# Pair 3 instead of pair 2 by the seven-product scheme, the second norm's last two sums on VectorE, and its root ahead of a conversion

## The chip, the cores and the metric

The kernel runs on one core of a Trainium2 chip. The metric is the device time of one execution in microseconds (us). TensorE multiplies, VectorE, ScalarE and GpSimd do elementwise work (the profile calls the four PE, DVE, ACT and POOL), and SyncE (SP) issues most DMAs.

## The reference

One layer on a sequence of 512 positions with 1024 features: a norm, one wide projection, a short gated convolution beside causal attention, a gated merge added to x, then a second norm and a channel mixer, and a last norm. The change lies where the merge ends and the mixer begins:

```python
x = x + (g_conv * y_conv + g_attn * y_attn) @ w_o[l]
h = rms_norm(x, norm_ffn_g[l])                 # the second norm
up = causal_dwconv(h @ w_up[l], conv_ffn_w[l]) # 1024 -> 2 * 2816, three taps per feature
a, b = jnp.split(up, 2, axis=-1)
x = x + (jax.nn.silu(a) * b) @ w_down[l]
```

## The kernel before, in words

Features lie on the 128 partitions, positions along the free axis, so x is eight blocks of 128 x 512. To hold float32 accuracy every operand is split into a high and a low part (names ending in h and l), and a product takes three matmuls: high by high, low by high, high by low. Matmuls are 128 x 128 by 128 x 256.

**Weights.** All weights come through one list of chunks, `stream`, in the order of their use. SyncE loads a chunk into one of five `raw` buffers. `split` makes the two parts: ScalarE copies it to `wh_...` (line 267), and VectorE subtracts to get `wl_...` (line 271). There are two buffers for each part, so a chunk is split while the chunk before it is multiplied. Behind each split `run_later` hands out work that waits in the list `later`.

**The up projection.** `w_up` gives 44 blocks of 128 features. Blocks `up(2j)` and `up(2j+1)` make pair j: the a half and the b half of 128 hidden features. A plain pair takes two chunks of 1024 columns and 48 matmuls for each. The pairs in `UPS`, 2 and 7, go another way: `up_pair` multiplies two by two blocks by a scheme with seven products instead of eight (table `PROD`), from four chunks P, F, P, F whose sums were formed ahead in DRAM by accumulating DMAs (names `sum`). That is 84 matmuls for the pair instead of 96, but VectorE has to combine four results (lines 1068 to 1073). It also needs sums of x's blocks ("forms"): `x1_sums` makes them from the tiles `xs2`, in the steps `t13` (lines 977, 978), `t24` (981, 982) and `hl` (985 on ScalarE, 986 on VectorE), which leave the forms' two parts in `xf`. The other line numbers of a pair: the norm's factor at 1091, three taps at 603 (ScalarE), 604 and 607 (VectorE) into `fu`, silu at 1101, the product of the halves on GpSimd at 1104 (even pairs, `ge`) or 1111 (odd, `go`). Behind an odd pair the forms for the down projection are made from `ge` and `go` (lines 1121 to 1131).

**The second norm.** As each block j of `x1` comes out of the product with `w_o` (`xr`, line 1001), it is split to `x1h` and `x1l` (1002, 1003), squared on ScalarE (`sq2`, 933) and added to `ssq2` by GpSimd (934). At the end `ssq2` is split in two, `s20` (1019) and `s21` (1020). Two pairs of matmuls by a block of ones, `pc_n2` (1253), sum over the features. They stand in the midst of the first two up blocks: in `lead`, block up0 runs up to its seventh of eight, up1 up to its second, then `mid` is called with those sums, then the rest. Then come the root (1257, ScalarE) and the reciprocal (1258, VectorE) that give `rb_n2`, by which every up block is multiplied.

**What sets the order.** A scheduler orders each engine's instructions, within the order written for TensorE, SyncE and for what `keep` marks. `after_split` holds instructions behind the last split. The order below is the one that came out.

Of the kernel before, what the change touches and what calls it, by code (L numbers as in the profile page):

```python
# [8 lines left out]
F32 = mybir.dt.float32  # L9
F32R = mybir.dt.float32r  # L10
AF = mybir.ActivationFunctionType
ALU = mybir.AluOpType

P = 128
D = 1024
S = 512
KB = D // P
NT = S // P
# [35 lines left out]
HELD = 2  # L54
GS = 2
NFF = len(STEPS[0]) + len(STEPS[1])
UPS = (2, 7)
NUP = NFF + 2 * (8 - GS)

PLAIN = [(m, k) for m in (6, 7) for k in range(*PHASES[1])]  # L60
# [4 lines left out]
def block_kernel(ctx, tc, xT, vecs, wv, win, wmix, wo, wup, wst, wdp, outT):  # L65
# [3 lines left out]
    nc = tc.nc  # L69
    PSUM = bass.MemoryType.PSUM  # L70

    cp = ctx.enter_context(tc.tile_pool(name="cp", bufs=1))
# [3 lines left out]
    def keep(ins):  # L76
        return tc.keep_in_program_order(ins)

    def bank(i, name):
        return ps.tile([P, S], F32, tag=f"b{i}", name=name)  # L80

    def ring(*ids):
        st = [0]

        def f(name):
            st[0] += 1
            return bank(ids[(st[0] - 1) % len(ids)], name)

        return f
# [107 lines left out]
    later = []  # L197
    held = [0]

    def after_split():  # L200

        st = ExitStack()
        for ins in order.values():
            st.enter_context(tc.issue_after(ins))
        return st
# [29 lines left out]
    def flush(banks=None):  # L235

        while any(banks is None or set(w[2]) & set(banks) for w in later):
            with after_split():
                later.pop(0)[3]()
# [50 lines left out]
    halves = [slice(0, S // 2), slice(S // 2, S)]  # L290
# [33 lines left out]
    ex = cp.tile([P, NT + 2], F32, tag="ex", name="ex")  # L324
    nc.gpsimd.memset(ex[:, :NT], -0.5)
    eps = ex[:, NT : NT + 1]
# [118 lines left out]
    ssq = ct("ssq1")  # L445
# [338 lines left out]
    acc, bank_s, bank_t = ring(2, 0, 1), ring(3, 4), ring(5, 6)  # L784
# [3 lines left out]
    for idx in late:  # L788
        kind, i = divmod(idx, 4)
# [29 lines left out]
    acc = ring(3, 4, 5, 6, 0, 1, 2, 7)  # L819
# [6 lines left out]
    mp = mg.enter_context(tc.tile_pool(name="mp", bufs=1))  # L826
# [56 lines left out]
    for j in range(KB):  # L883
# [28 lines left out]
        a, b = gs  # L912
# [9 lines left out]
    x1h = xp.tile([P, KB, S], F32R, tag="x1h", name="x1h")  # L922
    x1l = xp.tile([P, KB * S + PADR], F32R, tag="x1l", name="x1l")[:, : KB * S]
# [1 line left out]

    ssq2 = xp.tile([P, S], F32, tag="ssq", name="ssq2")

    def square_into(ssq, x, first, pool, name):
        if first:
            nc.scalar.activation(ssq, x, AF.Square)  # L930
        else:
            sq = pool.tile([P, S], F32, tag="sq", name=name)
            nc.scalar.activation(sq, x, AF.Square)
            nc.gpsimd.tensor_add(ssq, ssq, sq)

    def lead(names, xh, xl, mid=None, late=None):

        w = [chunk(n) for n in names]
        p = [acc(f"p_{n}") for n in names]

        def part(i, kbs):
            for kb in kbs:
                ks = slice(kb * P, (kb + 1) * P)
                mm3(p[i], w[i][0][:, ks], w[i][1][:, ks], xh[:, kb, :], xl[:, kb, :], kb == 0, kb == KB - 1)

        part(0, range(KB - 1))
        part(1, range(2))
        if mid is not None:
            mid()
        part(1, range(2, 4))  # L950
        part(0, (KB - 1,))
        part(1, range(4, KB))
        if late is not None:
            late()
        return p
# [37 lines left out]
    for j in range(KB):  # L993
        if j == 0:
            po = lead(["wo0", "wo1"], mh, ml)
        p = po[j] if j < 2 else block(f"wo{j}", mh, ml)
        for i in range(len(xr), min(j + 3, KB)):
            xr.append(mt(f"xr{i}"))
            nc.gpsimd.dma_start(xr[i], xT[:, i, :])
        y = xr[j]  # L1000
        nc.vector.tensor_add(y, p, y)
        nc.scalar.activation(x1h[:, j, :], y, AF.Copy, scale=col(G2 + j))
        nc.vector.scalar_tensor_tensor(
            x1l[:, j, :], y, col(G2 + j), x1h.bitcast(F32)[:, j, :], op0=ALU.mult, op1=ALU.subtract,
        )
        square_into(ssq2, y, j == 0, mp, f"sq2_{j}")
        nc.gpsimd.dma_start(x1d[:, j, :], y)
        q, i = divmod(j, 2)
        if i == 0:
            xs2 = mp.tile([P, 4, 2 * P], F32, tag="xs2", name=f"xs2{q}", bufs=2)  # L1010
        nc.scalar.activation(xs2[:, 2 * i : 2 * i + 2].rearrange("p h c -> p (h c)"), y, AF.Copy, scale=col(G2 + j))
        if i:
            x1_sums(q, xs2)
    n2 = [mp.tile([P, S], F32R, tag="s2", name=f"s2{i}", bufs=2) for i in range(2)]
    n2.append(mp.tile([P, P], F32R, tag="one", name="one"))
    hl = later.pop()
    flush()
    nc.scalar.activation(n2[2], ones, AF.Copy)
    nc.scalar.activation(n2[0], ssq2, AF.Copy)
    nc.vector.tensor_sub(n2[1], ssq2, n2[0].bitcast(F32))  # L1020
    later.append(hl)
    flush()
    mg.close()
    ab.close()

# [7 lines left out]
    gl = fp.tile([P, NG, 2 * P], F32R, tag="gl", name="gl")  # L1033
    halves_of = "p (h c) -> p h c"

    acc = ring(0, 1, 4, 5, 6, 7, 2, 3)
    ssq3 = xp.tile([P, S], F32, tag="ssq", name="ssq3")

    def place(ph, q):
# [41 lines left out]
    def up(j, rb2, pu=None):  # L1081
        uu = []
        if j in UPS:
            pu = up_pair(j)
        for s_ in range(2):
            p = pu[s_] if pu else block(f"up{2 * j + s_}", x1h, x1l, True)
            z = p if j <= UPS[-1] else fz(f"fz{j}{s_}")
            if s_ and j in UPS:
                nc.vector.scalar_tensor_tensor(z, p, -1.0, rb2, op0=ALU.mult, op1=ALU.mult)
            else:  # L1090
                nc.vector.tensor_mul(z, p, rb2)
            u = fp.tile([P, S], F32, tag="fu", name=f"fu{j}{s_}", bufs=3)
            taps(u, z, CF + 3 * (2 * j + s_))
            uu.append(u)
        return uu

    def glu(ph, j, uu):
        a, b = uu
        q, k = j // 2, len(parts) - 1
        g0 = place(ph, q)  # L1100
        nc.scalar.activation(a, a, AF.Silu)
        if j % 2 == 0:
            ge = glu.even = fp.tile([P, 2, 2 * P], F32, tag="ge", name=f"ge{q}", bufs=2)
            keep(nc.gpsimd.tensor_mul(ge, a.rearrange(halves_of, h=2), b.rearrange(halves_of, h=2)))  # L1104
            return
        flush()
        ge = glu.even
        go = fp.tile([P, 6, 2 * P], F32, tag="gr", name=f"go{q}")

        def mul(eng):  # L1110
            return eng.tensor_mul(go[:, 0:2, :], a.rearrange(halves_of, h=2), b.rearrange(halves_of, h=2))

        if j + 1 < PHASES[ph][1]:
            keep(mul(nc.gpsimd))
        else:
            later.append((k + 3, 0.7, (("q", q),), lambda: mul(nc.vector)))
        b11, b12 = ge[:, 0, :], ge[:, 1, :]
        b21, b22, t1, t2, t3, t4 = (go[:, i, :] for i in range(6))

        def t13():  # L1120
            nc.vector.tensor_sub(t1, b11, b12)
            nc.vector.tensor_sub(t3, b22, b12)

        def t24():
            nc.vector.scalar_tensor_tensor(t2, t1, -1.0, b22, op0=ALU.mult, op1=ALU.subtract)
            nc.vector.scalar_tensor_tensor(t4, t2, -1.0, b21, op0=ALU.mult, op1=ALU.subtract)

        def hl(src, gs):
            def f():
                nc.scalar.activation(gh[:, gs, :], src, AF.Copy)  # L1130
                nc.vector.tensor_sub(gl[:, gs, :], src, gh.bitcast(F32)[:, gs, :])

            return f


        d = (2, 3, 4) if j + 1 < PHASES[ph][1] else (4, 5, 6)
        w = [(d[0], 0.85, t13), (d[0], 0.85, t24), (d[1], 0.7, hl(ge[:, : 1 + ph, :], slice(g0, g0 + 1 + NF * ph, NF)))]
        w += [(d[x > 0 and 2 or 1], 0.7, hl(go[:, x : x + 2, :], slice(g0 + 1 + x, g0 + 3 + x))) for x in (0, 4, 2)]
        for n, us, f in w:
            later.append((k + n, us, (("q", q),), f))  # L1140
# [99 lines left out]
    for ph, (j0, j1) in enumerate(PHASES):  # L1240
        if ph:
            flush()
            acc = ring(*X)
        for j in range(j0, j1):
            pu = None
            if j == 0:
                nrm = {}

                def mid():
                    pc = bank(6, "pc_n2")  # L1250
                    for i, x in enumerate(n2[:2]):
                        for c, cs in enumerate(halves):
                            keep(nc.tensor.matmul(
                                pc[:, cs], n2[2], x[:, cs], start=i + c == 0, stop=i + c == 2
                            ))
                    rb2 = cp.tile([P, S], F32, tag="rb", name="rb_n2")
                    nc.scalar.activation(rb2, pc, AF.Sqrt, bias=eps, scale=1.0 / D)
                    nc.vector.reciprocal(rb2, rb2)
                    nrm["b"] = rb2

                pu = lead(["up0", "up1"], x1h, x1l, mid)
            glu(ph, j, up(j, nrm["b"], pu))
        down(ph, ph * len(STEPS[0]))


# [210 lines left out]
```

## Time and profile before

| | us |
|---|---|
| median of 3 runs | 697.64 (697.44 to 698.34) |
| profiled execution | 697.58 |
| its span, first to last instruction | 695.5 |
| TensorE busy | 685.4 |
| VectorE busy | 536.3 |
| ScalarE busy | 359.3 |
| GpSimd busy | 167.1 |
| TensorE's granted clock, of full speed | 0.997 |

The profile is of one execution. A row of the order of time gives the start from the span's beginning, the duration, the engine, the line, the operation, the tiles without their numbers, the shapes, the count, and in brackets the idle time ahead of it on its engine and what ended it. TensorE's matmuls overlap, so their starts say more than their durations.

### The profile page before, as it was taken

What the parts mean: (1) busy time and instruction counts of PE and PEld (TensorE: products, weight loads), DVE (VectorE), ACT (ScalarE), POOL (GpSimd) and SP (SyncE); (2) the same over time, 40 slices, a digit from 0 to 9 for tenths busy, and PEclk for the clock granted to TensorE, in tenths of its full rate; (3) what the DMA queues carried; (4) which work ended last, traced back from release to release, by engine and by line L of the source; (5) the groups of instructions that cost most, each with busy time, mean ns of one, the idle gap of its engine ahead of it and who ended that gap; (6) DMA issues with size and microseconds to landing.
All of it is one profiled execution on the core that took longest, in us unless ns stands there. A gap on an engine that the chain in (4) does not pass through costs nothing.

```text
span 695.5 us, 14650 instructions
## 1 busy us (share of the span) xinstructions
PE 685.4 (99%) x5952; PEld 682.6 (98%) x5952; DVE 536.3 (77%) x842; ACT 359.3 (52%) x570; POOL 167.1 (24%) x194
## 2 busy tenths in 40 slices
PE   9999999999999999999999999999999999999996
PEld 9999999999999999999999999999999999999996
DVE  6678777786687778769889869987684678777786
ACT  6664656554654444456654535545433354445663
POOL 5124745444021020224410231340000221131000
PEclk9999999999999999999999999999999999999998
DMA  8526957478489697878658467579967273544723
GB/s 309 194 82 225 208 140 182 98 181 180 125 213 289 215 259 206 242 249 258 176 116 281 104 147 263 172 190 263 261 200 228 92 175 117 134 105 129 197 84 121
DMA packets 59202, 128.87 MB, mean 185 GB/s; under 512 B 5344, under 2 KB 26848, under 8 KB 58880
## 3 DMA queue, kind: packets, MB, share of 16 engines
q1 hardware_dynamic: 41280, 100.22, 44.0%
q0 software_dynamic: 17136, 27.04, 21.9%
q8 instruction: 46, 0.75, 0.4%
q10 hardware_dynamic: 720, 0.69, 0.3%
q14 instruction: 20, 0.16, 0.1%
HBM read 123.67 MB, written 41.42 MB: 237 GB/s over the span
## 4 chain that ended last, share of the span: by engine, by line
PE 85%; DVE 7%; ACT 4%; issue 3%; DMA 1%; ACTq 0%; SPq 0%; DVEq 0%
PE p_up L300 21%; PE p_in L300 14%; PE dn L318 13%; PE gs L318 8%; PE p_up L318 7%; PE yc L318 3%; PE ya L300 3%; PE us L318 2%; PE p_g L300 2%; PE o L693 2%; PE pa L512 1%; PE pb L514 1%; PE tp L678 1%; PE p_wo L300 1%; PE pdB L300 1%
## 5 line engine op out<-in xcount | busy, mean ns | idle before, releaser
L300 PE MATMUL p_in<-xf,wh_in 128*128 128x256 f32 x576 | 95.7, 278 | 0.0
L300 PE MATMUL p_up<-x1l,wh_up 128*128 128x256 f32 x488 | 95.2, 276 | 0.0
L300 PE MATMUL p_up<-x1h,wh_up 128*128 128x256 f32 x488 | 95.0, 276 | 0.0
L300 PE MATMUL p_up<-x1h,wl_up 128*128 128x256 f32 x488 | 95.0, 276 | 0.0
L143 POOL DMA_DIRECT2D sum<-in_wst_dram x57 | 59.8, 1128 | 129.0 <-DMA sum<-sum 80.5
L300 PEld LDWEIGHTS p_in<-xf,wh_in 128*128 128x128 f32 x576 | 80.4, 188 | 0.7
L300 PEld LDWEIGHTS p_up<-x1l,wh_up 128*128 128x128 f32 x488 | 73.6, 188 | 0.0
L300 PEld LDWEIGHTS p_up<-x1h,wh_up 128*128 128x128 f32 x488 | 73.4, 188 | 0.0
L300 PEld LDWEIGHTS p_up<-x1h,wl_up 128*128 128x128 f32 x488 | 73.4, 188 | 0.0
L267 ACT ACTIVATE wh_up<-raw_up 128x1024 fp32r<-128x1024 f32 x40 | 42.3, 1058 | 58.9 <-PE p_up L300 49.4
L267 ACT ACTIVATE wh_F<-raw_F 128x1024 fp32r<-128x1024 f32 (+1 forms) x36 | 37.8, 1050 | 61.4 <-PE ya L300 25.8
L271 DVE TENSOR_TENSOR wl_F<-raw_F,wh_F 128x1024 fp32r<-128x1024 f32 (+1 forms) x36 | 45.2, 1256 | 21.7 <-ACT wh_F L267 21.5
L271 DVE TENSOR_TENSOR wl_up<-raw_up,wh_up 128x1024 fp32r<-128x1024 f32 x40 | 49.5, 1238 | 10.9 <-ACT wh_up L267 10.5
L300 PE MATMUL p_in<-xf,wl_in 128*128 128x256 f32 x288 | 56.6, 278 | 0.1
L1104 POOL TENSOR_TENSOR ge<-fu,fu 128x512 f32<-128x512 f32 x11 | 17.4, 1579 | 139.7 <-DVE fu L607 107.5
L267 ACT ACTIVATE wh_P<-raw_P 128x768 fp32r<-128x768 f32 (+1 forms) x36 | 30.0, 833 | 30.2 <-PE dn L318 15.0
L300 PEld LDWEIGHTS p_in<-xf,wl_in 128*128 128x128 f32 x288 | 43.5, 188 | 0.3 <-DVE wl_in L271 0.3
L271 DVE TENSOR_TENSOR wl_P<-raw_P,wh_P 128x768 fp32r<-128x768 f32 (+1 forms) x36 | 34.5, 957 | 9.8 <-PE gs L318 5.4
L318 PE MATMUL dn<-gl,wh_F 128*128 128x256 f32 x156 | 36.4, 276 | 0.0
L318 PE MATMUL dn<-gh,wh_F 128*128 128x256 f32 x156 | 36.3, 276 | 0.0
L318 PE MATMUL p_up<-x1h,wh_up 128*128 128x256 f32 x152 | 36.3, 276 | 0.0
L318 PE MATMUL p_up<-x1l,wh_up 128*128 128x256 f32 x152 | 36.3, 276 | 0.0
(351 smaller groups left out, 2015.2 us busy)
## 6 DMA issues: line engine op xcount, KB each, us to landing
raw_up<-in_wup_dram SPq DMA_DIRECT2D x40, 512.0 KB, 4.1
raw_F<-sum SPq DMA_DIRECT2D x35, 512.0 KB, 5.9
raw_P<-in_wst_dram SPq DMA_DIRECT2D x35, 384.0 KB, 3.9
raw_in<-in_win_dram SPq DMA_DIRECT2D x24, 512.0 KB, 3.7
sum<-in_wst_dram POOLq DMA_DIRECT2D x35, 256.0 KB, 5.5
sum<-in_wst_dram SPq DMA_DIRECT2D x17, 512.0 KB, 7.7
sum<-in_wst_dram POOLq DMA_DIRECT2D x17, 512.0 KB, 8.7
sum<-sum SPq DMA_DIRECT2D x34, 256.0 KB, 4.9
```

What stands on the lines that cost most here:

```text
L143: return lambda: keep(nc.gpsimd.dma_start(dst, src, accum_op=ALU.add))
L267: ins = nc.scalar.activation(hi, raw, AF.Copy)
L271: ins = nc.vector.tensor_sub(lo, raw, hi.bitcast(F32))
L300: keep(nc.tensor.matmul(out[:, cs], w, x[:, cs], start=start and i == 0 and c == 0, stop=stop and i == 2 and c == len(cut) - 1,))
L318: keep(nc.tensor.matmul(out, wl if x == 1 else wh, xl if x == 2 else xh, start=opens and bk not in seen, stop=closes and bk not in left,))
L512: keep(nc.tensor.matmul(pa[t][:, :VW], xt, w[:, :VW], start=start, stop=stop))
L514: keep(nc.tensor.matmul(pb[t], xt, w[:, VW:], start=start and t % 2 == 0, stop=stop and t % 2 == 1))
L678: keep(nc.tensor.transpose(tp[:, ks], pt[:, ks], ident))
L693: keep(nc.tensor.matmul(o[:, os_], vv[:, kb, pr, e, :], x[:, kb, cs], start=e == 0 and kb == 0 and i == 0, stop=e == 1 and kb == nk - 1 an ...
L1104: keep(nc.gpsimd.tensor_mul(ge, a.rearrange(halves_of, h=2), b.rearrange(halves_of, h=2)))
```

## The change

`UPS` becomes (3, 7). `square_into` takes an engine, which is GpSimd for blocks 1 to 5 and VectorE for 6 and 7. A root of one column of `s20` into a spare column of `ex` is added behind `s20`. The three last pieces of the forms (`t13`, `t24`, `hl` of the fourth group) are taken out of `later` and called by hand: `t13` first, then s21, then `t24`. The call of `lead` for the first two up blocks, with `mid`, moves ahead, then up2 is split, and `hl` comes last.

```diff
-UPS = (2, 7)
+UPS = (3, 7)
...
-    def square_into(ssq, x, first, pool, name):
+    def square_into(ssq, x, first, pool, name, eng):
...
-            nc.gpsimd.tensor_add(ssq, ssq, sq)
+            eng.tensor_add(ssq, ssq, sq)
...
-        square_into(ssq2, y, j == 0, mp, f"sq2_{j}")
+        square_into(ssq2, y, j == 0, mp, f"sq2_{j}", nc.gpsimd if j < KB - 2 else nc.vector)
...
-    hl = later.pop()
-    flush()
     nc.scalar.activation(n2[2], ones, AF.Copy)
     nc.scalar.activation(n2[0], ssq2, AF.Copy)
+    nc.scalar.activation(ex[:, NT + 1 :], n2[0].bitcast(F32)[:, :1], AF.Sqrt)
+    xf_last = [later.pop()[3] for _ in range(3)]
+    flush()
+    xf_last.pop()()
     nc.vector.tensor_sub(n2[1], ssq2, n2[0].bitcast(F32))
-    later.append(hl)
-    flush()
+    xf_last.pop()()
+    acc = ring(0, 1, 4, 5, 6, 7, 2, 3)
+    nrm = {}
+
+    def mid():
...
+    pu = lead(["up0", "up1"], x1h, x1l, mid)
+    split()
+    with after_split():
+        xf_last.pop()()
     mg.close()
     ab.close()
...
-                pu = lead(["up0", "up1"], x1h, x1l, mid)
-            glu(ph, j, up(j, nrm["b"], pu))
+            glu(ph, j, up(j, nrm["b"], None if j else pu))
```

How this moves the instructions is seen on two engines. In these rows the number behind a name's last underscore is the buffer's; shapes are partitions by elements.

First VectorE, where the squares' sum ends and up1 and up2 are split. Before:

```order
L977 TENSOR_TENSOR xs23_4500<-xs23_4500 128x256
L1001 TENSOR_TENSOR xr7_4423<-p_wo7_4511,xr7_4423 128x512
L271 TENSOR_TENSOR wl_up1_4599<-raw_up1_4365,wh_up1_4598 128x1024
L1003 SCALAR_TENSOR_TENSOR x1l_4032<-xr7_4423,vec_64,x1h_4031 128x512
L978 TENSOR_TENSOR xs23_4500<-xs23_4500 128x256
L981 SCALAR_TENSOR_TENSOR xs23_4500<-xs23_4500 128x256
L982 SCALAR_TENSOR_TENSOR xs23_4500<-xs23_4500 128x256
L1020 TENSOR_TENSOR s21_4569<-ssq2_4033,s20_4568 128x512
L986 TENSOR_TENSOR xf_110<-xs23_4500,xf_110 128x1024
L1258 RECIPROCAL rb_n2_4663<-rb_n2_4663 128x512
L271 TENSOR_TENSOR wl_up2_4725<-raw_up2_4433,wh_up2_4724 128x1024
```

Now, where lines 1022, 1036 and 934 are s21, the reciprocal and the add:

```order
L934 TENSOR_TENSOR ssq2_4033<-ssq2_4033,sq2_6_4496 128x512
L977 TENSOR_TENSOR xs23_4500<-xs23_4500 128x256
L1001 TENSOR_TENSOR xr7_4423<-p_wo7_4511,xr7_4423 128x512
L271 TENSOR_TENSOR wl_up1_4590<-raw_up1_4365,wh_up1_4589 128x1024
L1003 SCALAR_TENSOR_TENSOR x1l_4032<-xr7_4423,vec_64,x1h_4031 128x512
L934 TENSOR_TENSOR ssq2_4033<-ssq2_4033,sq2_7_4563 128x512
L978 TENSOR_TENSOR xs23_4500<-xs23_4500 128x256
L981 SCALAR_TENSOR_TENSOR xs23_4500<-xs23_4500 128x256
L1022 TENSOR_TENSOR s21_4569<-ssq2_4033,s20_4568 128x512
L982 SCALAR_TENSOR_TENSOR xs23_4500<-xs23_4500 128x256
L1036 RECIPROCAL rb_n2_4654<-rb_n2_4654 128x512
L271 TENSOR_TENSOR wl_up2_4703<-raw_up2_4433,wh_up2_4702 128x1024
```

Two adds have come in, s21 stands ahead of the second of the `t24` steps instead of behind it, and `xf` (line 986) has left its place ahead of the reciprocal; it now follows wl_up2 in the next row.

ScalarE at the same place, from the last of block 7's copies on. Before:

```order
L1011 ACTIVATE xs23_4500<-xr7_4423,vec_64 128x512
L1019 ACTIVATE s20_4568<-ssq2_4033 128x512
L985 ACTIVATE xf_110<-xs23_4500 128x1024
L1257 ACT_TABLE_LOAD
L1257 ACTIVATE rb_n2_4663<-pc_n2_4658,ex_103 128x512
L267 ACTIVATE wh_up2_4724<-raw_up2_4433 128x1024
L267 ACTIVATE wh_up3_4785<-raw_up3_4502 128x1024
```

Now:

```order
L1011 ACTIVATE xs23_4500<-xr7_4423,vec_64 128x512
L1017 ACTIVATE s20_4568<-ssq2_4033 128x512
L1018 ACT_TABLE_LOAD
L1018 ACTIVATE ex_103<-s20_4568 128x1
L1035 ACTIVATE rb_n2_4654<-pc_n2_4649,ex_103 128x512
L267 ACTIVATE wh_up2_4702<-raw_up2_4433 128x1024
L985 ACTIVATE xf_110<-xs23_4500 128x1024
L267 ACTIVATE wh_up3_4786<-raw_up3_4502 128x1024
```

The copy into `xf` was ahead of the table load and the root, and is now behind the root and wh_up2. The table load follows s20 and belongs to the added root of one column.

Last VectorE behind the pairs, where the low part of the fourth block after the pair is made. Behind pair 7, before (the same rows stand there now):

```order
L1091 TENSOR_TENSOR xg_5640<-p_up17_5721,rb_n2_4663 128x512
L1121 TENSOR_TENSOR go3_5658<-ge3_5506 128x256
L1122 TENSOR_TENSOR go3_5658<-go3_5658,ge3_5506 128x256
L1125 SCALAR_TENSOR_TENSOR go3_5658<-go3_5658 128x256
L271 TENSOR_TENSOR wl_up19_5847<-raw_up19_5590,wh_up19_5846 128x1024
L604 SCALAR_TENSOR_TENSOR fu81_5771<-xg_5640,vec_64,fu81_5771 128x511
L1126 SCALAR_TENSOR_TENSOR go3_5658<-go3_5658 128x256
L607 SCALAR_TENSOR_TENSOR fu81_5771<-xg_5640,vec_64,fu81_5771 128x510
```

Behind pair 3, now:

```order
L1110 TENSOR_TENSOR p_up9_5186<-p_up9_5186,rb_n2_4654 128x512
L1140 TENSOR_TENSOR go1_5123<-ge1_4974 128x256
L1141 TENSOR_TENSOR go1_5123<-go1_5123,ge1_4974 128x256
L1144 SCALAR_TENSOR_TENSOR go1_5123<-go1_5123 128x256
L604 SCALAR_TENSOR_TENSOR fu41_5236<-p_up9_5186,vec_64,fu41_5236 128x511
L1145 SCALAR_TENSOR_TENSOR go1_5123<-go1_5123 128x256
L607 SCALAR_TENSOR_TENSOR fu41_5236<-p_up9_5186,vec_64,fu41_5236 128x510
L271 TENSOR_TENSOR wl_up11_5312<-raw_up11_5058,wh_up11_5311 128x1024
```

Here wl_up11 stands behind both taps of fu41 and the last sum for go1, where wl_up19 stands ahead of the like steps.

More of the change, by code (lines that the diff above doesn't have):

```diff
@@ L1015, in block_kernel @@
     n2.append(mp.tile([P, P], F32R, tag="one", name="one"))
-    hl = later.pop()
-    flush()
     nc.scalar.activation(n2[2], ones, AF.Copy)
     nc.scalar.activation(n2[0], ssq2, AF.Copy)
+    nc.scalar.activation(ex[:, NT + 1 :], n2[0].bitcast(F32)[:, :1], AF.Sqrt)
+    xf_last = [later.pop()[3] for _ in range(3)]
+    flush()
+    xf_last.pop()()
     nc.vector.tensor_sub(n2[1], ssq2, n2[0].bitcast(F32))
-    later.append(hl)
-    flush()
+    xf_last.pop()()
+    acc = ring(0, 1, 4, 5, 6, 7, 2, 3)
+    nrm = {}
+    def mid():
+        pc = bank(6, "pc_n2")
+        for i, x in enumerate(n2[:2]):
+            for c, cs in enumerate(halves):
+                keep(nc.tensor.matmul(
+                    pc[:, cs], n2[2], x[:, cs], start=i + c == 0, stop=i + c == 2
+                ))
+        rb2 = cp.tile([P, S], F32, tag="rb", name="rb_n2")
+        nc.scalar.activation(rb2, pc, AF.Sqrt, bias=eps, scale=1.0 / D)
+        nc.vector.reciprocal(rb2, rb2)
+        nrm["b"] = rb2
+    pu = lead(["up0", "up1"], x1h, x1l, mid)
+    split()
+    with after_split():
+        xf_last.pop()()
     mg.close()
@@ L1034, in block_kernel @@
     halves_of = "p (h c) -> p h c"
-    acc = ring(0, 1, 4, 5, 6, 7, 2, 3)
     ssq3 = xp.tile([P, S], F32, tag="ssq", name="ssq3")
@@ L1244, in block_kernel @@
         for j in range(j0, j1):
[L1245 to L1259, printed above, removed]
-                pu = lead(["up0", "up1"], x1h, x1l, mid)
-            glu(ph, j, up(j, nrm["b"], pu))
+            glu(ph, j, up(j, nrm["b"], None if j else pu))
         down(ph, ph * len(STEPS[0]))
```

## The prediction

> **What bounds the kernel now.** I read the page's busy shares first, then who TensorE waits for, then its order of time at those places, and last the other engines there.
>
> ```profile
> PE 685.4 (99%) x5952; PEld 682.6 (98%) x5952; DVE 536.3 (77%) x842; ACT 359.3 (52%) x570; POOL 167.1 (24%) x194
> ```
> ```profile
> PE p_up L318 <- DVE wl_up L271: 1.9, 2, 1.1
> ...
> PE pc_n L1253 <- DVE s L1020: 0.6, 1, 0.6
> PE pc_n L1253 <- ACT s L1019: 0.4, 1, 0.4
> ```
>
> TensorE is busy for 99% of the span, so only its idle time can be won while its matmuls stay the same in number: the change gives it the same 84 matmuls per two by two pair and 96 per plain pair, in another order. The second fence lists all its waits but one at the start of the program. Four waits, 2.9 us by name, and all four lie in the stretch that the change rewrites. In order of time they are three gaps:
>
> ```profile
> 343.99 0.39 PE L300 MATMUL p_up<-x1l,wh_up 128*128 128x256 f32 x2
> 344.77 0.50 PE L1253 MATMUL pc_n<-s,one 128*128 128x256 f32 x2 [0.39 <-ACT s L1019]
> 345.93 0.50 PE L1253 MATMUL pc_n<-s,one 128*128 128x256 f32 x2 [0.65 <-DVE s L1020]
> 346.26 0.40 PE L300 MATMUL p_up<-x1h,wh_up 128*128 128x256 f32 x2
> ...
> 351.85 0.28 PE L318 MATMUL p_up<-x1l,wh_up 128*128 128x256 f32 x1
> 352.94 0.75 PE L318 MATMUL p_up<-x1h,wl_up 128*128 128x256 f32 x4 [0.82 <-DVE wl_up L271]
> 353.53 0.39 PE L300 MATMUL p_up<-x1h,wh_up 128*128 128x256 f32 x2
> 353.76 0.39 PE L300 MATMUL p_up<-x1h,wl_up 128*128 128x256 f32 x2
> ...
> 384.25 0.28 PE L318 MATMUL p_up<-x1l,wh_up 128*128 128x256 f32 x1
> 385.63 0.74 PE L318 MATMUL p_up<-x1h,wl_up 128*128 128x256 f32 x4 [1.10 <-DVE wl_up L271]
> 386.20 0.40 PE L300 MATMUL p_up<-x1h,wh_up 128*128 128x256 f32 x2
> ```
>
> Undisturbed, a row of two follows the last by 0.227 us (353.53 to 353.76, and so in 4.08 us for 36), so a matmul takes a slot of 0.113. From that each gap is priced by starts, which is more than the "idle" in brackets. Gap A, the norm's sums: the next slot after 343.99 is 344.22, four matmuls of 0.113 would end at 344.67, and p_up resumed at 346.26: 1.59 us. Gap B, the low part of up2: slot 351.96, four matmuls to 352.41, resumed at 353.53: 1.12 us. Gap C, the low part of up8: slot 384.36, to 384.81, resumed at 386.20: 1.39 us. Together 4.10 us, 0.59% of the span.
>
> **What holds gaps A and B.** The same stretch on GpSimd, VectorE and ScalarE:
>
> ```profile
> 338.28 1.58 POOL L934 TENSOR_TENSOR ssq<-ssq,sq 128x512 f32<-128x512 f32 x1 [0.52 <-ACT sq L933]
> 342.21 1.84 POOL L934 TENSOR_TENSOR ssq<-ssq,sq 128x512 f32<-128x512 f32 x1
> ```
> ```profile
> 337.95 0.75 DVE L1003 SCALAR_TENSOR_TENSOR x1l<-xr,vec,x1h 128x512 fp32r<-128x512 f32 x1
> 338.83 1.31 DVE L977 TENSOR_TENSOR xs<-xs 128x256 f32<-128x256 f32 x1
> 340.06 0.68 DVE L1001 TENSOR_TENSOR xr<-p_wo,xr 128x512 f32<-128x512 f32 x1
> 340.67 1.21 DVE L271 TENSOR_TENSOR wl_up<-raw_up,wh_up 128x1024 fp32r<-128x1024 f32 x1
> 341.80 0.74 DVE L1003 SCALAR_TENSOR_TENSOR x1l<-xr,vec,x1h 128x512 fp32r<-128x512 f32 x1
> 342.67 1.68 DVE L978 TENSOR_TENSOR xs<-xs 128x256 f32<-128x256 f32 x1
> 344.38 0.42 DVE L981 SCALAR_TENSOR_TENSOR xs<-xs 128x256 f32<-128x256 f32 x1
> 345.19 0.68 DVE L1020 TENSOR_TENSOR s<-ssq,s 128x512 fp32r<-128x512 f32 x1
> 348.45 3.35 DVE L1258 RECIPROCAL rb_n<-rb_n 128x512 f32<-128x512 f32 x1 [0.78 <-ACT rb_n L1257]
> 351.72 1.16 DVE L271 TENSOR_TENSOR wl_up<-raw_up,wh_up 128x1024 fp32r<-128x1024 f32 x1
> ```
> ```profile
> 344.09 0.63 ACT L1019 ACTIVATE s<-ssq 128x512 fp32r<-128x512 f32 x1 [1.45 <-POOL ssq L934]
> 345.36 1.06 ACT L985 ACTIVATE xf<-xs 128x1024 fp32r<-128x1024 f32 x1 [0.64 <-DVE xs L982]
> 346.44 1.28 ACT L1257 ACT_TABLE_LOAD   x1
> 347.73 0.69 ACT L1257 ACTIVATE rb_n<-pc_n,ex 128x512 f32<-128x512 f32 x1
> ```
>
> The sum of squares is ready at 344.05, when GpSimd's second add ends; ScalarE copies it (s20) at once. VectorE can take s21 only behind all of xs23's sums, at 345.19. Then ScalarE converts xf, loads a table, takes the root (347.73); the reciprocal follows, and wl_up2 stands behind its 3.27 us.
>
> **The change, part by part.** *Adds of VectorE instead of GpSimd.* GpSimd loses 1.58 and 1.84 us. VectorE's price for the same tile is in the trace, from the first norm:
>
> ```profile
> L480 DVE TENSOR_TENSOR ssq<-ssq,sq x7: 682/687/694, 11.0 to 22.0; 128x512 f32<-128x512 f32 x7
> L977 DVE TENSOR_TENSOR xs<-xs x4: 420/1312/1675, 305.9 to 338.8; 128x256 f32<-128x256 f32 x4
> L1238 ACT ACTIVATE ex<-ex 128x1 f32<-128x1 f32 x1 | 0.2, 203 | 0.0
> ```
>
> So VectorE gains two of 0.69. It also loses something: line 977 takes 0.42 us undisturbed and 1.31 beside GpSimd's add, ending 0.28 after the add does; line 978 took 1.68. Without the adds I take 0.42 for both, 2.15 us less against 1.37 more. The Trainium skill, page "SBUF — State Buffer", section "SBUF: two separate sides", says that a VectorE operation with two SBUF inputs and a GpSimd operation that reads SBUF take a shared port pair as an exclusive lock, the later one waiting. The trace agrees: 977 ends only after 339.86, where the add ends, though at 340.14, sooner than a whole 0.42 behind it. By rule or row the sum is the same, as no GpSimd operation on SBUF is left in that stretch.
>
> I now lay out the new order from 338.70, the end of x1l for block 6, each VectorE step starting 0.08 before the printed end of the last (340.67 against 340.74). Add 339.31; line 977 339.65; xr7 340.25; wl_up1 341.38; x1l7 342.04; add 342.65. ScalarE copies s20 to 343.32. VectorE does 978 and 981 meanwhile (343.33), then s21 to 344.04. TensorE, unchanged, wants s20 at 344.22 and s21 at 344.45: 0.9 and 0.4 us to spare. Gap A closes: **-1.59**, of which between nothing and all could come back if VectorE slips by 0.4 to 2 us.
>
> *Root ahead of xf.* ScalarE's table load now follows s20 (343.33 to 344.61), pulled forward by a root of one column, 0.20 us (row of line 1238). The norm's matmuls end at 344.67 plus 0.16 of the last one's length (0.28 less its slot), so the root runs 344.87 to 345.56 and the reciprocal to 348.93, 2.9 us earlier than before. wh_up2's buffer is free when p_up0's last block is through (18 matmuls after 344.67, 346.7), and its 1.06 us (xf's row, same form) end by 347.9; wl_up2 runs 348.85 to 350.01. TensorE wants it after the 42 matmuls left of p_up0 and p_up1 and 8 of up2, at 350.33, its weight load 0.11 earlier: 0.2 us to spare. Gap B closes, but barely: **-1.12, of which I give back 0.1** (bounds: 0, and the whole 1.12 if the reciprocal starts 1.3 us later than I have it).
>
> *xf's lower part behind wl_up2.* Its 1.2 us (wl_up's form) now stand ahead of wl_up3, which ends about 353.5 (wl_up2, xf, two products of 0.69, itself). TensorE wants it at 349.43 + 48 + 8 slots = 355.8: 2.3 us cover it, and beyond that each us late would cost one. xf itself is first read by the pair, now behind up5 at about 371, 20 us after it is written.
>
> *Pair 3 in place of pair 2.* What holds gap C, and the one pair that stands in an odd place already, pair 7:
>
> ```profile
> 383.62 1.95 DVE L271 TENSOR_TENSOR wl_up<-raw_up,wh_up 128x1024 fp32r<-128x1024 f32 x1
> ...
> 424.98 1.23 DVE L271 TENSOR_TENSOR wl_up<-raw_up,wh_up 128x1024 fp32r<-128x1024 f32 x1 [0.20 <-ACT wh_up L267]
> ...
> 440.87 1.21 DVE L271 TENSOR_TENSOR wl_up<-raw_up,wh_up 128x1024 fp32r<-128x1024 f32 x1
> ```
> ```profile
> 383.20 1.29 POOL L1104 TENSOR_TENSOR ge<-fu,fu 128x512 f32<-128x512 f32 x1 [14.01 <-ACT fu L1101]
> ```
> ```profile
> 427.08 0.28 PE L318 MATMUL p_up<-x1h,wh_up 128*128 128x256 f32 x1
> ```
>
> After pair 2 VectorE owes the pair's sums, the forms of blocks 0 and 1 and five taps before wl_up8, which starts only at 383.62 and is stretched from 1.22 to 1.95 by GpSimd's product at 383.20. Of the four low parts after pair 7 the first ends at 426.21 and the fourth, up19's, at 442.08. The blocks start at 427.08 and every 48 slots (5.44 us) later and want theirs 8 slots in: the first at 427.99, the fourth at 444.3. So 1.8 and 2.2 us are spare, with the same debts on VectorE. The new order behind pair 3 is pair 7's, except that its fourth, wl_up11, stands behind two more taps and a sum, some 1.65 us by starts: 0.5 us are left. Gap C closes: **-1.39**. Pair 7 and all behind it keep their order.
>
> *Costed at nothing.* SyncE loads raw_up4 and raw_up5 where raw_P32 and raw_F32 were, from 330 and 338 on for blocks that start after 360. GpSimd's DMA for sum12 goes ahead of product ge0 instead of behind it: one issue near 343, with ge0 not due before 355. The copies of sum10 and sum11 move up SyncE's queue (rival below).
>
> Sum: 1.59 + 1.12 - 0.1 + 1.39 = 4.0. The profiled execution took 697.58 us (span 695.5 and 2.1 around it), 0.06 below the median; 697.64 - 4.0 = **693.6**. The slower steps behind a gap (0.40 against 0.39 at 386.20) might give 0.1 more.
>
> **Rivals.** *The reciprocal stays last.* VectorE's two adds or line 978 slip, so half of A or most of B remains: about 1.0 us back, 694.6. For it: spare times of 0.2 and 0.4 us; against: the adds' price is a row.
> *Gap C moves behind pair 3.* A GpSimd product of 1.3 us starts just ahead of wl_up11 or wl_up12 and stretches it by 0.73, as at 383.62, with only 0.5 to spare, or VectorE is further behind than after pair 7: up to 1.4 back, 695.0. The Trainium skill's lock rule (page "SBUF — State Buffer", the same section) gives such a collision wherever GpSimd is first.
> *No change that shows.* The closed gaps reopen later, at blocks that now have little to spare: within 0.2%, about 697.
> *Slower.* SyncE's copy of sum10 now stands ahead of raw_F33 and waits for GpSimd's accumulating DMA, issued near 341.
>
> ```profile
> DMA to landing us min/median/max: 4.4/7.2/11.8
> ```
>
> The pair starts near 371 and reads F33 after 60 of its 84 slots, at 378, so raw_F33 must be issued by some 369, with a median 7.2 us to land and 1.06 for its conversion. The add would have to land 28 us after its issue to delay TensorE at all, and past 373 to eat the 4.0 us; at 374.5 the time is 699.1. The row's longest is 11.8.
>
> **Chances.** Forecast 0.66; reciprocal last 0.12; gap moved 0.13; no change 0.05; slower 0.04. All but the last two are beyond 0.2% (1.4 us, about what a measurement of this kernel can tell from no change): faster 0.91, same 0.05, slower 0.04. The forecast's own range is 693.2 to 694.2; with the two partial cases, 693.0 to 695.4.
>
> **What would show it.** Right: no wait of pc_n; s21 ended near 344.0 and the root near 345.6; lines 977 and 978 at 0.42; wl_up2 ended before 350.3; no wait on wl_up8 to wl_up12. Wrong: a reciprocal that starts after 346, a low part over 1.9 us behind pair 3, or SyncE idle on sum10.

## The result, and the profile after

| | before | after |
|---|---|---|
| median, us | 697.55 (697.38 to 699.38, 6 runs) | 693.46 (693.11 to 693.93, 6 runs) |
| profiled execution, us | 697.58 | 693.39 |
| its span, us | 695.5 | 691.4 |

The ratio is 0.9936, with a 95% interval of 0.9923 to 0.9949: 4.09 us less, 0.6%. The forecast was 693.6.

The page's busy shares, then the first line of its chain of work that ended last (before, that line began "PE 85%; DVE 7%; ACT 4%"), then the whole list of what TensorE waits for:

```profile
PE 684.3 (99%) x5952; PEld 682.7 (99%) x5952; DVE 534.1 (77%) x844; ACT 359.0 (52%) x571; POOL 165.7 (24%) x192
...
PE 96%; DVE 2%; ACT 1%; issue 1%; ACTq 0%; DVEq 0%
```
```profile
PE warm L108 <- DVE ones L100: 1.1, 1, 1.1
```

TensorE does the same 5952 matmuls. The four waits of before are gone, and what is left is the one at the start. TensorE's order of time where gaps A and B were:

```profile
343.96 0.39 PE L300 MATMUL p_up<-x1l,wh_up 128*128 128x256 f32 x2
344.18 0.64 PE L1031 MATMUL pc_n<-s,one 128*128 128x256 f32 x4
344.66 0.40 PE L300 MATMUL p_up<-x1h,wh_up 128*128 128x256 f32 x2
...
350.27 0.28 PE L318 MATMUL p_up<-x1l,wh_up 128*128 128x256 f32 x1
350.38 0.62 PE L318 MATMUL p_up<-x1h,wl_up 128*128 128x256 f32 x4
350.84 0.39 PE L300 MATMUL p_up<-x1h,wh_up 128*128 128x256 f32 x2
```

The four matmuls of the norm are now one row, and each row starts in its slot. VectorE and ScalarE in the same stretch:

```profile
338.58 0.69 DVE L934 TENSOR_TENSOR ssq<-ssq,sq 128x512 f32<-128x512 f32 x1
339.18 0.42 DVE L977 TENSOR_TENSOR xs<-xs 128x256 f32<-128x256 f32 x1
...
342.51 0.42 DVE L978 TENSOR_TENSOR xs<-xs 128x256 f32<-128x256 f32 x1
...
343.31 0.68 DVE L1022 TENSOR_TENSOR s<-ssq,s 128x512 fp32r<-128x512 f32 x1
...
345.58 3.35 DVE L1036 RECIPROCAL rb_n<-rb_n 128x512 f32<-128x512 f32 x1 [1.25 <-ACT rb_n L1035]
348.85 1.16 DVE L271 TENSOR_TENSOR wl_up<-raw_up,wh_up 128x1024 fp32r<-128x1024 f32 x1
```
```profile
342.63 0.64 ACT L1017 ACTIVATE s<-ssq 128x512 fp32r<-128x512 f32 x1 [0.53 <-DVE ssq L934]
343.29 1.28 ACT L1018 ACT_TABLE_LOAD   x1
344.58 0.20 ACT L1018 ACTIVATE ex<-s 128x1 f32<-128x1 f32 x1
344.86 0.69 ACT L1035 ACTIVATE rb_n<-pc_n,ex 128x512 f32<-128x512 f32 x1
```

Lines 977 and 978 are down from 1.31 and 1.68 to 0.42, s21 ends at 343.99, 0.42 us before its slot at 344.41, and the reciprocal starts 2.87 us earlier than before. In and behind pair 3, the last low part of the pair itself and the four behind it on VectorE, the three products of GpSimd near them, and TensorE's first use of the fourth low part behind the pair:

```profile
376.38 2.07 DVE L271 TENSOR_TENSOR wl_F<-raw_F,wh_F 128x1024 fp32r<-128x1024 f32 x1 [0.44 <-ACT wh_F L267]
378.65 1.22 DVE L271 TENSOR_TENSOR wl_up<-raw_up,wh_up 128x1024 fp32r<-128x1024 f32 x1 [0.19 <-ACT wh_up L267]
382.27 1.22 DVE L271 TENSOR_TENSOR wl_up<-raw_up,wh_up 128x1024 fp32r<-128x1024 f32 x1
387.97 1.23 DVE L271 TENSOR_TENSOR wl_up<-raw_up,wh_up 128x1024 fp32r<-128x1024 f32 x1
...
395.83 1.21 DVE L271 TENSOR_TENSOR wl_up<-raw_up,wh_up 128x1024 fp32r<-128x1024 f32 x1
```
```profile
376.09 1.29 POOL L1123 TENSOR_TENSOR ge<-fu,fu 128x512 f32<-128x512 f32 x1 [9.80 <-DVE fu L607]
...
392.00 1.30 POOL L1130 TENSOR_TENSOR go<-fu,fu 128x512 f32<-128x512 f32 x1 [14.62 <-DVE fu L607]
...
396.05 2.14 POOL L1123 TENSOR_TENSOR ge<-fu,fu 128x512 f32<-128x512 f32 x1 [1.76 <-ACT gh L1149]
```
```profile
397.98 0.62 PE L318 MATMUL p_up<-x1h,wl_up 128*128 128x256 f32 x4
```

None of the four behind the pair is stretched. The fourth, wl_up11, ends at 397.04, 0.9 us before it is used. GpSimd's product at 396.05 started 0.22 us behind it, and was itself the one that took 2.14 instead of 1.30. Within the pair a low part did meet a product, `ge` at 376.09, and took 2.07 us. It ended at 378.45, and TensorE used it only at 379.85, so it cost nothing.

### The profile page after: what moved, and what is told of

It is laid out like the page before. It is cut to its first block, busy times and chain, and to the rows that moved or that the text cites. A ratio compares the mean times of both kernels' runs of the same rounds, so it can differ in the third digit from the quotient of the medians.

```text
span 691.4 us, 14653 instructions
## 1 busy us (share of the span) xinstructions
PE 684.3 (99%) x5952; PEld 682.7 (99%) x5952; DVE 534.1 (77%) x844; ACT 359.0 (52%) x571; POOL 165.7 (24%) x192
## 4 chain that ended last, share of the span: by engine, by line
PE 96%; DVE 2%; ACT 1%; issue 1%; ACTq 0%; DVEq 0%
PE p_up L300 24%; PE p_in L300 14%; PE dn L318 13%; PE gs L318 8%; PE p_up L318 7%; PE p_wo L300 6%; PE yc L318 3%; PE ya L300 3%; PE us L318 3%; PE pa L512 2%; PE pb L514 2%; PE p_g L300 2%; PE o L693 2%; PE tp L678 1%; PE pdB L300 1%; PE pdA L300 1%
```

## The experiments

Each run is compared with runs of the kernel before on the same chip. The intervals are of the ratio to these.

**The two halves.** Pair 3 alone, on the kernel before:

```diff
-UPS = (2, 7)
+UPS = (3, 7)
```


> The kernel before with only the two by two pair moved from place 2 to place 3; squares' sums and root as before. Theory of three separate gaps: gap C (1.39 us at up8) closes, gaps A and B (1.59 and 1.12 us) stay, so about 696.1 us; the low parts behind pair 3 end as behind pair 7. Rival, that the place doesn't matter and VectorE is as late behind any pair: gap C comes back at up10 or up11 and the time stays within 0.3 us of 697.5.

695.91 us, 0.9977 (0.9968 to 0.9985): 1.7 less by medians. Gap C is gone, and A and B stand as before (idle times of 0.39, 0.65 and 0.82 us). And all but that, the kernel after with pair 2:

```diff
-UPS = (3, 7)
+UPS = (2, 7)
```


> The changed kernel with the pair put back to place 2, so only the norm's parts of the change. Theory of separate gaps: A and B closed, C as before, about 697.55 - 2.7 + 0.1 = 694.9 us, wl_up8 again late and stretched to some 1.95 us. Rival, that gap C was a late effect of the norm's stretch (VectorE's backlog carried on from there): C shrinks too, and the time is 693.5 to 694.2 us.

694.85 us, 0.9962 (0.9950 to 0.9975): 2.7 less. TensorE's only gap is C, behind a low part that GpSimd's product met 0.43 us after its own start (GpSimd, then VectorE):

```profile
380.63 1.29 POOL L1123 TENSOR_TENSOR ge<-fu,fu 128x512 f32<-128x512 f32 x1 [13.90 <-ACT fu L1120]
```
```profile
381.06 1.95 DVE L271 TENSOR_TENSOR wl_up<-raw_up,wh_up 128x1024 fp32r<-128x1024 f32 x1
```

Both halves bring what their gaps were priced at (1.39 and 2.71 us) to 0.3 us, and together, 4.4 us, they make up the change's 4.09 within what the runs resolve: the intervals are 1.2 to 1.8 us wide.

**The norm's half in two.** Only the adds on VectorE, on the kernel before:

```diff
-    def square_into(ssq, x, first, pool, name):
+    def square_into(ssq, x, first, pool, name, eng):
...
-            nc.gpsimd.tensor_add(ssq, ssq, sq)
+            eng.tensor_add(ssq, ssq, sq)
...
-        square_into(ssq2, y, j == 0, mp, f"sq2_{j}")
+        square_into(ssq2, y, j == 0, mp, f"sq2_{j}", nc.gpsimd if j < KB - 2 else nc.vector)
```


> The kernel before with only the last two adds of squares on VectorE; xf still ahead of the table load and the root, pair at place 2. Theory: lines 977 and 978 fall to 0.42 us, gap A closes (1.59 us), but the root stays behind xf (343.9 + 0.42 for the last sum, xf to 345.4, table to 346.7, root to 347.4, reciprocal to 350.7, wl_up2 to 351.8 against a want at 350.4), so gap B grows to about 1.5 us: gain 1.2 us, 696.3 us. Rival, that GpSimd's adds held nothing that TensorE waits for in the end: A moves wholly into B, 697.5 us.

696.89 us (695.92 to 698.89 in 11 runs), 0.9991 (0.9982 to 1.0000). The size is unclear: the median lies 0.6 above what was expected and the runs scatter. The trace, of the fastest run, shows the mechanism, but not the size: TensorE is at the norm's sums 0.6 us sooner there than in the kernel after (343.59 against 344.18), which was won ahead of the place that this edit touches. TensorE at A and at B:

```profile
343.59 0.64 PE L1253 MATMUL pc_n<-s,one 128*128 128x256 f32 x4
...
351.41 0.72 PE L318 MATMUL p_up<-x1h,wl_up 128*128 128x256 f32 x4 [1.46 <-DVE wl_up L271]
```

A is closed, but B's idle time has grown from 0.82 to 1.46: TensorE is at up2 sooner, while xf's conversion still stands ahead of the root. By starts B is 1.73 us, 0.61 more than before, which leaves 0.98 of A's 1.59. The spans of eight of the eleven runs, 694.6 to 694.9 where before was 695.5, fit that. Only the new order and the early root, with the adds left on GpSimd and pair 2, that is, in the kernel after:

```diff
-UPS = (3, 7)
+UPS = (2, 7)
...
-        square_into(ssq2, y, j == 0, mp, f"sq2_{j}", nc.gpsimd if j < KB - 2 else nc.vector)
+        square_into(ssq2, y, j == 0, mp, f"sq2_{j}", nc.gpsimd)
```


> The kernel before with the root, its early table load and the new order of xf, but all adds of squares on GpSimd and the pair at place 2. Theory: s20 still ends only at 344.7 and s21 at about 345.4, so gap A keeps about 1.1 of its 1.59 us; root at 346.2 to 346.9, reciprocal to 350.2, wl_up2 to 351.3 against a want at 351.4: gap B closes. Gain 1.5 to 1.6 us, 696.0 us. Rival, that the two halves are worth something only together: under 0.5 us, 697.1 us or more.

696.35 us, 0.9980 (0.9971 to 0.9989): 1.2 less than before, where 1.5 was expected. B is closed. A stands whole, as TensorE's, GpSimd's and VectorE's rows show:

```profile
344.88 0.50 PE L1031 MATMUL pc_n<-s,one 128*128 128x256 f32 x2 [0.39 <-ACT s L1017]
346.03 0.50 PE L1031 MATMUL pc_n<-s,one 128*128 128x256 f32 x2 [0.65 <-DVE s L1022]
```
```profile
342.32 1.84 POOL L934 TENSOR_TENSOR ssq<-ssq,sq 128x512 f32<-128x512 f32 x1
```
```profile
342.78 1.68 DVE L978 TENSOR_TENSOR xs<-xs 128x256 f32<-128x256 f32 x1
...
344.95 0.43 DVE L982 SCALAR_TENSOR_TENSOR xs<-xs 128x256 f32<-128x256 f32 x1
345.29 0.68 DVE L1022 TENSOR_TENSOR s<-ssq,s 128x512 fp32r<-128x512 f32 x1
```

Line 978 ends only at 344.46, behind GpSimd's add (344.16). And s21 hasn't moved: it can't start before s20 is through at 344.82, and the scheduler has put it behind both `t24` steps, as before. In the run with the adds alone it stands ahead of line 982 (342.71 and 343.31), though that edit orders nothing. So A hangs on where the adds are and B on the order, and the adds without the order give 0.6 of their 1.6 us back at B.

**The early root.** Without it, else the kernel after:

```diff
-    nc.scalar.activation(ex[:, NT + 1 :], n2[0].bitcast(F32)[:, :1], AF.Sqrt)
```


> The changed kernel without the added root of one column; everything else the same. If a table load waits with the instruction that needs it (as the load ahead of the first silu seemed to, at 357.26 right behind the tap it needs), it starts only when the norm's matmuls end at 344.83: root at 346.1 instead of 344.86, wl_up2 1.26 us later with 0.3 us to spare, gap B opens to about 1.0 us, 694.4 us. If the load runs ahead of that wait, it starts behind s20 at 343.3 as now, root at 344.9, 693.5 us: the added root does nothing.

693.35 us, 0.9945 (0.9932 to 0.9957): as the kernel after. ScalarE:

```profile
343.42 1.28 ACT L1034 ACT_TABLE_LOAD   x1
344.99 0.69 ACT L1034 ACTIVATE rb_n<-pc_n,ex 128x512 f32<-128x512 f32 x1 [0.29 <-PE pc_n L1030]
```

The table load runs right behind s20 (which ends at 343.40), though the root that it belongs to waits for the norm's sums until 344.99. By the order of ScalarE's rows, what let it go early is that xf's conversion no longer stands ahead of it. That a load runs ahead of such a wait isn't so everywhere. In the kernel before, the load ahead of the first silu began only when the tap that the silu needs was through:

```profile
357.26 1.28 ACT L1101 ACT_TABLE_LOAD   x1 [2.42 <-DVE fu L607]
```

So the first theory of this run had a row for it, and the second came true at this place. What decides between the two is not shown.

**GpSimd beside VectorE again.** The kernel after, with the same squares also added on GpSimd into a tile that nothing reads:

```diff
+    idle = abp.tile([P, 2, S], F32, tag="xq", name="idle", bufs=2)[:, 0, :]
+    nc.gpsimd.memset(idle, 0.0)
...
+            if eng is nc.vector:
+                nc.gpsimd.tensor_add(idle, idle, sq)
```


> The changed kernel, and GpSimd adds the last two squares as well, into a tile that nothing reads. No data depends on these adds except that the square's buffer is free later. Theory that GpSimd's add and VectorE's operations with two inputs in SBUF hold each other off: line 977's like stretches from 0.42 to about 1.0, VectorE's second add of squares ends about 344.1 instead of 342.6, s21 about 345.6, gap A opens by 1.2 us, gap B stays shut (the root is not later than TensorE): about 694.7 us. Rival, that the adds were late only because GpSimd is slower (1.58 against 0.69 us): no change, 693.5 us.

696.28 us, 0.9979 (0.9970 to 0.9988), in two groups near 695.6 and 697.1; the profiled run is of the lower one. By the median 2.8 us come back, in the lower group some 2.1, both more than either theory gave. Gap A in the trace is 2.34 us by starts (slot 344.56, resumed 347.35 behind four matmuls); what the upper group lost besides has no trace. VectorE's own adds, GpSimd's, and TensorE at A:

```profile
338.96 1.80 DVE L936 TENSOR_TENSOR ssq<-ssq,sq 128x512 f32<-128x512 f32 x1
...
343.41 2.15 DVE L936 TENSOR_TENSOR ssq<-ssq,sq 128x512 f32<-128x512 f32 x1
```
```profile
338.62 1.59 POOL L938 TENSOR_TENSOR idle<-idle,sq 128x512 f32<-128x512 f32 x1 [0.52 <-ACT sq L935]
...
343.16 1.83 POOL L938 TENSOR_TENSOR idle<-idle,sq 128x512 f32<-128x512 f32 x1
```
```profile
346.27 0.50 PE L1035 MATMUL pc_n<-s,one 128*128 128x256 f32 x2 [1.55 <-ACT s L1021]
```

The add takes 1.80 and 2.15 us instead of 0.69 wherever GpSimd's began 0.3 us before it, and both delays add up on VectorE (1.11 + 1.46). The expectation counted one. The Trainium skill's lock rule ("SBUF — State Buffer", section "SBUF: two separate sides") would let VectorE's add run whole behind GpSimd's, to 340.90 and 345.68; it ended at 340.76 and 345.56, so it blocks as the rule says but for a tenth or so at the end. So with GpSimd still adding in the stretch the adds' move brings nothing. The run does not show that the slower add was harmless: in the kernel before, GpSimd's second add was the first of the two to start, at 342.21, and its 1.84 us are what s20 waited for, while the stretched line 978 is what s21 waited for.

**How near the reciprocal is.** Two operations without effect ahead of it, in the kernel after:

```diff
         nc.scalar.activation(rb2, pc, AF.Sqrt, bias=eps, scale=1.0 / D)
+        for _ in range(2):
+            nc.vector.tensor_tensor(rb2, rb2, rb2, op=ALU.max)
         nc.vector.reciprocal(rb2, rb2)
```


> The changed kernel with two operations on 128x512 that change no value (the larger of a tile and itself) ahead of the reciprocal, 0.69 us each and one behind the other, so about 1.35 us. Theory that wl_up2 ends only some 0.3 us before TensorE wants it: gap B opens to about 1.05 us, 694.5 us. Rival, that there is more room there than the order of time shows: no change, 693.5 us.

694.57 us, 0.9957 (0.9943 to 0.9970): 1.1 more than after. VectorE and TensorE:

```profile
347.13 3.35 DVE L1038 RECIPROCAL rb_n<-rb_n 128x512 f32<-128x512 f32 x1
350.40 1.16 DVE L271 TENSOR_TENSOR wl_up<-raw_up,wh_up 128x1024 fp32r<-128x1024 f32 x1
```
```profile
351.62 0.74 PE L318 MATMUL p_up<-x1h,wl_up 128*128 128x256 f32 x4 [0.97 <-DVE wl_up L271]
```

The two cost VectorE 1.45 us by starts, and TensorE resumes 1.14 behind its slot (350.48): the spare time at B is 0.3 us.

**Which places are good.** Pair 4 instead of pair 3, in the kernel after:

```diff
-UPS = (3, 7)
+UPS = (4, 7)
```


> The changed kernel with the first two by two pair at place 4 (even) instead of 3. Theory that the gap belongs to an even place, because the forms of the odd pair ahead and the pair's own debts then fall together on VectorE: a gap of 1 to 1.5 us opens at the third block behind pair 4, 694.5 to 695.0 us. Rival, that place 2 was bad because it is close behind the norm, with VectorE still behind: place 4 is as good as 3, 693.5 us.

694.93 us, 0.9962 (0.9950 to 0.9975). The gap is back at full size (1.11 idle, as behind pair 2), 22 us later in the program, with the same meeting (GpSimd, VectorE):

```profile
402.38 1.29 POOL L1123 TENSOR_TENSOR ge<-fu,fu 128x512 f32<-128x512 f32 x1 [11.96 <-ACT fu L1120]
```
```profile
402.80 1.96 DVE L271 TENSOR_TENSOR wl_up<-raw_up,wh_up 128x1024 fp32r<-128x1024 f32 x1
```

So nearness to the norm is not what made gap C. Two things make it, at both places. VectorE comes to the low part of the third block behind the pair only when the pair's debts are done: TensorE's slot is 403.53 here, and a low part of 1.22 us begun at 402.80 would have ended 0.5 us late without any meeting (behind pair 2, 383.62 against a slot of 384.36, the same). And the pair's own product, `ge`, started just ahead of it, adds 0.7. Behind pair 3 VectorE makes that low part ahead of most of the taps, at 387.97 for a slot at 392.54, and the pair's `go`, at 392.00, falls between two low parts. No run separates the two causes.

**A third pair.** Pairs 3, 7, 11 and pairs 3, 5, 7, with more DMA steps handed out so that the sums come in time:

```diff
-UPS = (3, 7)
+UPS = (3, 7, 11)
...
-            if nm[0] in "m":
+            if nm[0] in "mw" or nm in ("up0", "up1", "up2", "up3", "up4", "up5"):
```


> The changed kernel with a third two by two pair at place 11, UPS = (3, 7, 11), and with the sums of its weights formed while w_o and the first up blocks run, two DMA steps behind a split as elsewhere. It does 12 matmuls less than the kernel after, in exchange for the pair's sums on VectorE and four more accumulating DMAs. Theory (an odd place with plain pairs ahead of it lets VectorE catch up, so a pair costs its matmuls alone): 12 slots of 0.113 us less, 693.46 - 1.36 = 692.1. Rival 1 (pair 11 shuts no gap, because pair 7's debts and its own come too close, or a GpSimd product falls on a low part behind it): a gap of 1.1 to 1.4 us as behind pair 2 or 4, 693.2 to 693.5. Rival 2 (the added DMAs hold up the first chunks of up): a wait of TensorE on wh or wl before pair 3, 694 or more.

> As the run with pairs 3, 7 and 11, but with pairs 3, 5 and 7: one plain pair of 10.9 us lies between two by two pairs. The matmuls are as few as there, so by TensorE alone it is 692.1. Theory: VectorE is what limits a pair's place; between pairs it has to do the debts of a pair and all of a plain pair's work before the next pair's low parts, and the trace after shows its last low part behind a pair with 0.9 us to spare after two plain pairs, so here it is late: a gap of 1 to 3 us behind pair 5 and again behind pair 7, 693.5 to 697. Rival (only the parity of the place counts, since that is what decides whether GpSimd's product falls on a low part): no gap, 692.1.

696.14 us, 0.9970 (0.9959 to 0.9981), and 696.26 us, 0.9977 (0.9968 to 0.9986). In both, two chunks of the down projection are read before the last add into their sums, so part of that product is another than the reference's; instructions and bytes are the same. With 3, 5, 7, TensorE is late four times, by 0.47 to 0.70 us a time by starts, less than the theory's 1 to 3 and from pair 7 on. Three times VectorE's low part is late, as the theory said. The first of these, at the start of pair 7, was stretched from 0.95 to 1.75 us by the `go` of pair 5, so an odd place does not keep clear of such a meeting. The fourth is a wait for an accumulator. At the end of the down projection TensorE is 1.8 us behind the kernel after; the other 1.0 us of the 2.8 between the two spans lies behind it. With 3, 7, 11, none of the theories held. The only gap is at the start of the down projection (TensorE, VectorE, and by stretches of time: busy time of the engines, then the granted clock, the DMA share and GB/s):

```profile
465.42 0.28 PE L318 MATMUL dn<-gl,wh_P 128*128 128x256 f32 x1
467.61 0.39 PE L318 MATMUL dn<-gh,wh_P 128*128 128x256 f32 x1 [1.92 <-DVE uz L1087]
```
```profile
466.00 1.22 DVE L271 TENSOR_TENSOR wl_F<-raw_F,wh_F 128x1024 fp32r<-128x1024 f32 x1
467.13 0.42 DVE L1087 TENSOR_TENSOR uz<-us,uz 128x256 f32<-128x256 f32 x1
```
```profile
467.00:469.00 2.00, 1.37 (x6) 1.16 (x7) 1.83 (x5) 0.00 (x0) 1.07 (x1) 0.78 1.09 314
469.00:471.00 2.00, 2.00 (x11) 2.00 (x11) 2.00 (x4) 0.75 (x1) 0.00 (x0) 0.50 1.01 395
```

The ring of accumulators gives pair 11 two that the down projection uses first, and they come free only with the sums of line 1087, which stand behind a low part on VectorE: 2.08 us by starts. Behind that idle time the clock was granted at half, 11 matmuls in 2 us, and 1.9 us more were lost: from 468.1 to 471.5, some 3.4 us, single matmuls follow one another by 0.21 us instead of 0.113. Four of the seven runs, 696.1 to 696.5, have a mean granted clock of 0.994 or 0.995, and three, 694.1 to 694.9, have 0.997: the forecast of 692.1 and the 2.1 us of the gap would give 694.2, so these three seem to have kept the clock, but no trace of one is at hand. The same with another order of the ring, and with the DMA steps handed out further, against the kernel after:

```diff
-    acc = ring(0, 1, 4, 5, 6, 7, 2, 3)
+    acc = ring(0, 1, 4, 5, 2, 3, 6, 7)
...
-            if nm[0] in "m":
+            if nm[0] in "mw" or nm[0] == "u" and int(nm[2:]) < 16:
```


> Pairs 3, 7 and 11 again, with two edits. The ring of accumulators for up becomes (0, 1, 4, 5, 2, 3, 6, 7), so that pair 11 stands in 4, 5, 2, 3 and the down projection's first product finds 6, 7, 0, 1 free; and all plain blocks up to up13 hand out a second DMA step, so that every sum is whole before it is loaded. In the run with pairs 3, 7 and 11 the only gap from 300 us on was at the start of the down projection: its third matmul stood 2.1 us behind its slot, waiting for VectorE's first sum (uz) of pair 11 to free the accumulator, and behind it the granted clock was at 0.50 for some 2 us, which took 1.8 us more. Theory (only those two cost, and both come from the accumulators): 12 slots of 0.113 less than the kernel after, and at most 0.5 us of small waits for low parts behind pair 11, where VectorE is full: 692.1 to 692.6. Rival (VectorE's debts behind pair 11 are what is late, whoever waits for them): the gap moves to the second or third chunk of the down projection, 1 to 2 us, and with an idle time of 1.9 us or more the clock falls again: 693.5 to 695.5.

693.70 us (693.06 to 696.10), 0.9957 (0.9944 to 0.9971). The gap and the slow clock are gone, and the largest idle time of TensorE behind the pair is this:

```profile
475.18 0.36 PE L318 MATMUL dn<-gh,wh_P 128*128 128x256 f32 x1 [0.32 <-ACT wh_F L267]
```

The profiled run took 693.06. By starts of matmuls from 371 us on, 1.36 us less of matmuls stand against 1.0 us of delays in the first chunks of the down projection, where 0.5 was allowed. VectorE is busy there for all but 0.13 of the 10 us from 465 on. So accumulators and clock were what cost 696.14, as the theory had it, but the third pair is worth 0.3 us in that run, and by the medians it is not faster than the kernel after. The median lies where the rival had it, without the rival's gap: what the theory had too low are the small delays. Why some runs are above 695 no trace here shows.

## Why the prediction was right

**The sum.** 4.10 us of gaps less 0.1 were forecast. Measured are 4.09 by medians and 4.19 between the profiled executions. That it came so near is in part luck: the interval is 1.8 us wide, and the two halves measured apart give 4.4. Whether the 0.1 held back for gap B was needed the times can't tell; the trace shows no wait there. The slower rows that the prediction mentioned are there: the ten rows behind gap C take 0.08 us longer than undisturbed ones.

**Gap A.** s20 ended at 343.27 (forecast 343.32), s21 at 343.99 (344.04). The run with the adds alone closes A, so the adds are enough for it, and the run with GpSimd beside VectorE shows that they are so only where GpSimd is away, as the prediction had it. No run shows how the 1.59 us are shared between GpSimd's slower add and the rows of VectorE that it stretched.

**Gap B.** The reciprocal ended at 348.93, as forecast, and wl_up2 ran at the forecast 348.85 to 350.01. The spare time, forecast at 0.2, is 0.3 by the delayed reciprocal. What was wrong is one cause: the prediction had the table load "pulled forward by a root of one column". It goes as early without that root. The term kept its size, since by ScalarE's order it is xf's move that frees the table load.

**Gap C.** No low part was late. The term that was mis-sized is the spare time of wl_up11, 0.9 us where 0.5 was forecast. The meeting that the rival feared was missed by 0.22 us: that is how much earlier wl_up11 started than GpSimd's product. By these 0.9 us it would have cost hardly anything even so, as the stretch is 0.7; a gap of 1.4 us, as behind pairs 2 and 4, needs a VectorE that is 0.5 us late besides.

**Costed at nothing.** In the changed kernel SyncE issued sum10's copy at 353.92 and sum11's at 358.28 without a wait, so the slower rival had nothing to stand on.

## What to carry to other kernels

Where one engine is busy for 99%, list its waits, price each by the starts of its rows and not by the idle time named, and ask of each what stands ahead of the late instruction on its engine: here three gaps were priced at 4.10 us together and brought 4.09, and each half came within 0.3 us of its price. A stretched row points to a neighbour: VectorE took over GpSimd's two adds and had less to do by it. Before adding work that saves matmuls, look at what frees its accumulators and who stands in that queue: the 1.36 us that twelve matmuls saved stood against 4.0 us for one late sum, half of it by the clock.

## What the runs showed of the hardware that was not expected

- One idle time of 1.92 us was followed by a granted clock of 0.50 for some 3.4 us (468.1 to 471.5; 11 matmuls in 469 to 471, where 2 us hold some 18), while in the traces idle times of 1.46 us (adds alone) and 1.55 us (GpSimd beside VectorE) left it at 1.00. The Trainium skill ("TensorE: Matmul & The Clock Gate", section "What's actually happening") has the half rate follow an idle window of about 3.4 us; the rate agrees, and here a shorter idle time did it, in the one trace that shows it. The times say more without a trace: three of the seven runs of that kernel have a mean clock of 0.997, so it need not happen, and four of the five slowest runs of GpSimd beside VectorE have 0.995 or 0.996 where the others have 0.997 or 0.998, so that 1.55 us may not be safe either.
- ScalarE's table load can run ahead of the operand of the instruction that needs it: without the early root it ran from 343.42 to 344.70, and its root waited until 344.99. It need not: ahead of the first silu of the kernel before, a load began at 357.26, behind 2.42 us of idle time that a tap ended.
- Behind the norm's four matmuls five rows of two follow one another by 0.24 us instead of 0.227 even where nothing waits (344.66 to 345.85 in the kernel after), 0.05 us in all.
